# Longer estimates of when an attention task's results are there

## The chip, the cores and the metric
One core of a Trainium2 chip runs the whole program. The metric is device time in microseconds (us) of one execution. The engines are TensorE (PE, with its weight loads PEld), VectorE (DVE), ScalarE (ACT), GpSimd (POOL) and SyncE (SP, which issues most transfers); each takes its own instructions in order and waits where a result of another is not there yet.

## The reference
One transformer layer on 256 latent tokens and 256 context tokens, width 2048, in float32. What is computed:

```
h = rms_norm(x)*(1+sc_a)+sh_a;   hc = the same of the context           # adaLN modulation from c
p = h @ w_in                                                            # 2048 x 4928, split by head group
NA   (4 heads): neighbourhood attention with a bias, plus the context
GQA  (4 heads): q, k normed and rotated, 2 k/v heads
MLA  (4 heads): q = norm(cq) @ w_uq, k, v = norm(ckv) @ w_ukv, rotary part apart
DIFF (4 heads): softmax(q1 k1) - lam * softmax(q2 k2), times v, rms_norm per head
x = x + gt_a * (concat(heads) @ w_out)
x = x + gt_f * ((silu(h2 @ wg) * (h2 @ wu)) @ wd),  h2 = modulated norm of x
out = rms_norm(x)
```

## The kernel before
Every large product runs as three matmuls on split operands: `whi` is the weight cast on ACT (line 142), `wlo` the rest from DVE (line 145), and `mm3s` (lines 165, 166, 168) adds hi·hi, hi·lo and lo·hi into a PSUM tile `acc`. The weights come through eight buffers `raw`, issued by SP at line 128. The same eight buffers also carry rows of `w_ada` for the later modulation vectors (`mod_tasks`), which DVE sums at line 380.

Small work is written as Python generators, called tasks, and laid between these matmuls by the class `Side`, a planner that works when the program is built. It keeps a clock `now`. A task yields a cost and a wait: the planner moves `now` by the cost and takes up the task again only when `now` has passed the wait, its estimate of how long the other engines need. `pump(cost)` is called after each group of 12 large matmuls (some 2.6 on that clock), and steps the tasks that are due. `finish(tasks)` steps tasks until those named are done, with no large matmul written between. The framework then orders each engine's instructions by its own model and may draw a few later matmuls forward.

The order of the stage: the projections of NA and GQA in blocks; then `proj` for ML_CQ and DF_Q while the NA and GQA heads run as tasks `attend` (scores, softmax `soft`, transposes of `p` at line 607, product with v at line 658); `finish(*gq_tasks)` at line 814; `proj` for ML_CKV; the MLA up-projections `mla_up`; `proj` for DF_K; `finish(*ml_tasks)` at line 932; `proj` for DF_V; then the first twelve row blocks of `w_out` while the four DIFF heads run as tasks `diff`; `finish(*df_tasks)` at line 977; `split_o(3)`, which makes `o_hi3` (ACT, line 946) and `o_lo3` (DVE, line 947) of the DIFF heads' output; then the last four row blocks of `w_out`, which read them, and the second norm.

In `diff`, after the product with v (line 913), the result is squared (ACT 915), summed (DVE 917), turned into a factor (DVE 175, POOL 177), scaled (DVE 921) into `tok`, transposed (PE 607) and copied with the gain (ACT 923). `gq_prep` (lines 700 to 743) makes the rotated and normed q and k of GQA: the last two k tiles are transposed at line 607 and copied at line 742 into `gq_kT`, which the scores at line 748 read.

```
def finish(self, *tasks):
    ...
        self.now = max(self.now, best["ready"])
        self._step(best)
```

Of the kernel before, what the change touches and what calls it, by code (L numbers as in the profile page):

```python
# [87 lines left out]
def hybrid_dit_kernel(ctx: ExitStack, tc: tile.TileContext, a, out):  # L88
# [28 lines left out]
    def misc():  # L117
        return psM.tile([P, 512], F32, name="m")
# [61 lines left out]
    def tsl(t):  # L180
        return slice(t * P, (t + 1) * P)
# [393 lines left out]
    def tok():  # L575
        return at.tile([P, 512], F32, name="tok", bufs=4)
# [27 lines left out]
    def transposes(dst, src, n, evac=None):  # L604
        ps = misc()
        for j in range(n):
            pe.transpose(ps[:, tsl(j)], src[:, tsl(j)], ident)  # L607
        v = ps[:, :n * P].rearrange("p (j n) -> p j n", j=n)
        if evac is None:
            act.copy(dst, v)  # L610
        else:
            evac(dst, v)
# [16 lines left out]
    def soft(score, bias=None):  # L629

        if bias is not None:
            dve.tensor_tensor(out=score[:, 0:S], in0=score[:, 0:S], in1=bias, op=ALU.add)
        st = small.tile([P, 4], F32, name="st")
        dve.tensor_reduce(out=st[:, 0:1], in_=score, axis=AX.X, op=ALU.max, negate=True)
        p = at.tile([P, 512], F32, name="p", bufs=3)
        act.activation(p, score, AF.Exp, bias=st[:, 0:1], accum_out=st[:, 1:2])
        dve.reciprocal(st[:, 2:3], st[:, 1:2])
        return p, st[:, 2:3]

    def attend(h, g, score_mm, vt, v0, bias=None):  # L640
        pT = at.tile([P, 4, S], F32, name="pT", bufs=2)
        ps_ = []
        for t in range(2):
            sc = misc()
            score_mm(sc, h, t)
            p, r = soft(sc, None if bias is None else bias(h, t))
            if t < 1:
                act.activation(p, p, AF.Copy, scale=r)
            else:
                dve.tensor_scalar(out=p, in0=p, scalar1=r, scalar2=None, op0=ALU.mult)  # L650
            ps_.append(p)
            yield 0.9, (1.0 if t == 0 else 3.0)
        for t in range(2):
            transposes(pT[:, :, tsl(t)], ps_[t], 4)
            yield 0.43, (0.5 if t == 0 else 2.0)
        o = misc()
        for kc in range(4):
            pe.matmul(o[:, :S], lhsT=vt(kc)[:, v0:v0 + P], rhs=pT[:, kc, :], start=(kc == 0), stop=(kc == 3))  # L658
        act.copy(o_tile(g // 4)[:, g % 4, :], o[:, :S])
        yield 1.7, 0.0  # L660
# [45 lines left out]
    def gq_prep():  # L706
        q = {}
        yield 0.0, 3.0
        for t in range(2):
            r = head_rstd(gq_q[:, t, :], 4)  # L710
            q[t] = tok()
            rope(q[t], gq_q[:, t, :], tabs["q"][0][:, t, :], tabs["q"][1][:, t, :], 4, 128)
            qv = q[t].rearrange("p (h d) -> p h d", h=4)
            for h in range(4):
                dve.tensor_scalar(out=qv[:, h, :], in0=qv[:, h, :], scalar1=r[:, h:h + 1], scalar2=None, op0=ALU.mult)
            yield 0.0, 3.0
        gq_T["q"] = qtile()
        for t in range(2):
            transposes(gq_T["q"][:, :, tsl(t)], q[t], 4, scaled(128.0 ** -0.5))
            yield 0.43, 0.5  # L720
        k = {}
        for w in range(2):
            k[w] = tok()
            for i in range(2):
                t = 2 * w + i
                kw = k[w][:, i * S:(i + 1) * S]
                r = head_rstd(gq_k[:, t, :], 2)
                src = gq_k[:, t, :]
                if w == 0:
                    rope(kw, src, tabs["k"][0][:, t, :], tabs["k"][1][:, t, :], 2, 128)  # L730
                    src = kw
                for h in range(2):
                    dve.tensor_scalar(out=kw[:, tsl(h)], in0=src[:, tsl(h)], scalar1=r[:, h:h + 1], scalar2=None, op0=ALU.mult)
                yield 0.0, 2.0
        gq_T["k"] = kv.tile([P, 2, NT], F32, name="gq_kT", tag="gk")
        for t in range(4):
            src = k[t // 2][:, (t % 2) * S:(t % 2 + 1) * S]
            dst = gq_T["k"][:, :, tsl(t)]
            if t < 2:
                transposes(dst, src, 2)  # L740
            else:
                transposes(dst, src, 2, lambda d, v: act.activation(d, v, AF.Copy, scale=colB[:, 33:34]))
            yield 0.21, 0.5

    gq_ready = side.add(gq_prep(), lane="e", width=4)

# [27 lines left out]
    def cq_evac(t, ps):  # L774
        r = row_rstd(ps, 512)
        q = tok()
        dve.scalar_tensor_tensor(out=q, in0=ps, scalar=r[:, 0:1], in1=gcq, op0=ALU.mult, op1=ALU.mult)
        yield 0.0, 7.0
        transposes(None, q, 4, split_evac(cqT, tsl(t)))
        yield 0.43, 0.0  # L780

    def ckv_evac(t, ps):
        r = row_rstd(ps[:, 0:256], 256)
        k = tok()
        dve.scalar_tensor_tensor(out=k[:, 0:256], in0=ps[:, 0:256], scalar=r[:, 0:1], in1=gckv, op0=ALU.mult, op1=ALU.mult)
        if t < 2:
            rope(k[:, 256:320], ps[:, 256:320], c64[:, t, :], s64[:, t, :], 1, 64)
            dve.tensor_copy(k[:, 320:384], k[:, 256:320])
        else:
            act.copy(k[:, 256:320], ps[:, 256:320])  # L790
            act.copy(k[:, 320:384], ps[:, 256:320])  # L791
        yield 0.0, 7.0
        transposes(None, k, 2, split_evac(ckvT, tsl(t)))
        transposes(kpeT[:, tsl(t)].unsqueeze(1), k[:, 256:384], 1)
        yield 0.32, 0.0
# [4 lines left out]
    def dq_evac(t, ps):  # L800
        q = tok()
        rope(q, ps, c64[:, t, :], s64[:, t, :], 8, 64)
        yield 0.0, 7.0
        transposes(df_qT[:, :, tsl(t)], q, 4, scaled(0.125))
        yield 0.43, 0.0

# [60 lines left out]
    def dk_evac(t, ps):  # L867
        k = tok()
        if t < 2:
            rope(k, ps, c64[:, t, :], s64[:, t, :], 8, 64)  # L870
        else:
            act.copy(k, ps)
        yield 0.0, 7.0 if t < 2 else 2.0
        ps_ = misc()
        for j in range(4):
            pe.transpose(ps_[:, tsl(j)], k[:, tsl(j)], ident)
        for i in range(2):
            act.copy(df_kT[i][:, :, tsl(t)], ps_[:, i * S:(i + 1) * S].rearrange("p (j n) -> p j n", j=2))
        yield 0.43, 0.0
# [10 lines left out]
    def diff(h):  # L890
        pT = at.tile([P, 4, S], F32, name="pT", bufs=2)
        for t in range(2):
            ps_, rs_ = [], []
            for i in range(2):
                sc = misc()
                hb = slice(64 * i, 64 * i + 64)
                pe.matmul(sc, lhsT=df_qT[hb, h, tsl(t)], rhs=df_kT[h // 2][hb, h % 2, :], start=True, stop=True)  # L897
                p, r = soft(sc)
                ps_.append(p)
                rs_.append(r)  # L900
            yield 1.7, 0.5
            l1 = small.tile([P, 1], F32, name="l1")
            dve.tensor_tensor(out=l1, in0=rs_[1], in1=neglam, op=ALU.mult)
            dve.tensor_scalar(out=ps_[1], in0=ps_[1], scalar1=l1, scalar2=None, op0=ALU.mult)
            dve.scalar_tensor_tensor(out=ps_[0], in0=ps_[0], scalar=rs_[0], in1=ps_[1], op0=ALU.mult, op1=ALU.add)
            yield 0.0, 3.0 + 1.0
            transposes(pT[:, :, tsl(t)], ps_[0], 4)
            yield 0.43, 2.0 if t else 0.5
        vt = df_v["v"]
        o = misc()  # L910
        for t in range(2):
            for kc in range(4):
                pe.matmul(o[:, tsl(t)], lhsT=pT[:, kc, tsl(t)], rhs=vt[:, kc, tsl(h)], start=(kc == 0), stop=(kc == 3))  # L913
        sq = at.tile([P, 512], F32, name="ropet")
        act.activation(sq[:, :S], o[:, :S], AF.Square)
        ss = small.tile([P, 8], F32, name="ss")
        dve.tensor_reduce(out=ss[:, :2], in_=sq[:, :S].rearrange("p (h d) -> p h d", h=2), axis=AX.X, op=ALU.add)
        r = rstd_of(ss[:, :2], 2, P)
        od = tok()
        for t in range(2):  # L920
            dve.tensor_scalar(out=od[:, tsl(t)], in0=o[:, tsl(t)], scalar1=r[:, t:t + 1], scalar2=None, op0=ALU.mult)
        yield 1.7, 4.0
        transposes(o_tile(3)[:, h, :].rearrange("p (t n) -> p t n", t=2), od, 2, lambda d, v: act.activation(d, v, AF.Copy, scale=gsub))
        yield 0.21, 0.0

# [317 lines left out]
```

## Time and profile before

| | |
|---|---|
| time, median of 3 runs | 1356.57 us (1356.53 to 1358.23) |
| the profiled execution | 1355.29 us |
| its span, first to last instruction | 1353.5 us |
| PE busy | 1324.0 us, 98% |
| DVE busy | 923.2 us, 68% |
| ACT busy | 625.7 us, 46% |

The profile is of one execution; 1.8 us of its time lie outside its span. "Busy" of PE holds the pipelined end of each matmul, so short waits hide in it; the start times in a timeline show them. The blocks of attention tasks stand between 240 and 580 us of the span.

### The profile page before, as it was taken

Reading aid. Unit: us, or ns where it says so; the run is one execution under the profiler, and the core shown is the slowest. Engines: PE = TensorE matmul, PEld = TensorE weight load, DVE = VectorE, ACT = ScalarE, POOL = GpSimd, SP = SyncE. Lnnn points to the kernel's source line nnn. Section 1 sums busy time; section 2 is a strip of 40 time slices with the busy share of each in tenths; the row PEclk is TensorE's granted clock in tenths of the full one; section 3 lists DMA queues with packets and bytes.
Section 4 is the critical chain, followed back from the end, with each engine's and each line's share of the span. In section 5 each row is a group of like instructions: output and inputs, shape, how many; then the busy total and the mean of one; then the engine's idle time right before and its main releaser. Section 6 shows DMA issues by size and latency. Waiting matters only on the chain.

```text
span 1353.5 us, 21027 instructions
## 1 busy us (share of the span) xinstructions
PE 1324.0 (98%) x7018; PEld 1077.5 (80%) x7018; DVE 923.2 (68%) x1687; ACT 625.7 (46%) x1183; POOL 99.6 (7%) x159
## 2 busy tenths in 40 slices
PE   6999999999999999999999999999999999999997
PEld 4788888778886777777888888888888888888886
DVE  4577789998679747778887954445555566556565
ACT  4532343564334435557445444444444444444453
POOL 1110000100000000000322200001001000011000
PEclk9999999999999999999999999999999999999999
DMA  9999996586687756455999855567667655676553
GB/s 367 344 356 323 322 364 220 171 268 213 198 262 262 247 166 212 135 184 164 344 368 340 307 191 192 193 196 219 210 212 228 218 193 185 203 226 224 193 178 129
DMA packets 190161, 322.29 MB, mean 238 GB/s; under 512 B 22466, under 2 KB 62436, under 8 KB 189028
## 3 DMA queue, kind: packets, MB, share of 16 engines
q1 hardware_dynamic: 177568, 285.28, 63.8%
q0 software_dynamic: 9136, 32.53, 6.5%
q10 hardware_dynamic: 3348, 3.13, 0.7%
q8 instruction: 55, 0.90, 0.3%
q14 instruction: 54, 0.44, 0.1%
HBM read 314.56 MB, written 6.31 MB: 237 GB/s over the span
## 4 chain that ended last, share of the span: by engine, by line
PE 68%; DVE 1%; ACT 1%; DMA 0%; issue 0%; POOL 0%; POOLq 0%; DVEq 0%; SPq 0%; ACTq 0%
PE acc L165 21%; PE acc L168 21%; PE acc L166 21%; PE m L862 1%; PE m L607 1%; PE m L861 1%; PE m L913 1%; PE m L897 1%; PE m L658 1%; DVE wlo L145 0%; PE m L165 0%; PE m L166 0%; PE m L168 0%; ACT whi L142 0%; DMA raw<-in_w_out_dram 0%; PE m L385 0%
## 5 line engine op out<-in xcount | busy, mean ns | idle before, releaser
L145 DVE TENSOR_TENSOR wlo<-raw,whi 128x512 fp32r<-128x512 f32 (+1 forms) x764 | 490.4, 680 | 286.0 <-ACT whi L142 281.5
L142 ACT CAST whi<-raw 128x512 fp32r<-128x512 f32 (+1 forms) x764 | 437.6, 615 | 520.2 <-PE acc L166 427.5
L165 PE MATMUL acc<-whi,h_hi 128*128 128x512 f32 x704 | 274.2, 390 | 0.7 <-ACT h_hi L1013 0.7
L166 PE MATMUL acc<-whi,h_lo 128*128 128x512 f32 x704 | 274.1, 389 | 0.4 <-DVE h_lo L1014 0.4
L168 PE MATMUL acc<-wlo,h_hi 128*128 128x512 f32 x704 | 190.8, 390 | 0.0
L165 PE MATMUL acc<-whi,h 128*128 128x512 f32 (+1 forms) x416 | 161.6, 392 | 1.2 <-ACT tok L791 0.5
L166 PE MATMUL acc<-whi,h 128*128 128x512 f32 (+1 forms) x416 | 157.1, 379 | 0.0
L168 PEld LDWEIGHTS acc<-wlo,h_hi 128*128 128x128 f32 x704 | 132.1, 188 | 28.5 <-DVE wlo L145 1.2
L165 PEld LDWEIGHTS acc<-whi,h_hi 128*128 128x128 f32 x704 | 132.2, 188 | 28.2 <-ACT h_hi L1013 1.1
L166 PEld LDWEIGHTS acc<-whi,h_lo 128*128 128x128 f32 x704 | 132.2, 188 | 28.0 <-DVE h_lo L1014 0.7
L165 PE MATMUL acc<-whi,ah 128*128 128x512 f32 (+1 forms) x364 | 139.1, 384 | 0.0
L166 PE MATMUL acc<-whi,al 128*128 128x512 f32 (+1 forms) x364 | 138.6, 382 | 0.0
L380 DVE SCALAR_TENSOR_TENSOR ada_acc<-raw,cs,ada_acc 128x512 f32<-128x512 f32 x135 | 100.9, 747 | 21.7 <-DMA raw<-in_w_ada_dram 20.2
L168 PE MATMUL acc<-wlo,h 128*128 128x512 f32 (+1 forms) x416 | 114.5, 379 | 1.1 <-DVE wlo L145 1.0
L168 PE MATMUL acc<-wlo,ah 128*128 128x512 f32 (+1 forms) x364 | 96.2, 382 | 0.0
L165 PEld LDWEIGHTS acc<-whi,h 128*128 128x128 f32 x416 | 78.0, 188 | 19.2 <-issue 3.7
L166 PEld LDWEIGHTS acc<-whi,h 128*128 128x128 f32 x416 | 78.2, 188 | 13.4 <-issue 1.2
L168 PEld LDWEIGHTS acc<-wlo,h 128*128 128x128 f32 x416 | 75.9, 188 | 16.2 <-DVE wlo L145 2.5
L165 PEld LDWEIGHTS acc<-whi,ah 128*128 128x128 f32 x364 | 68.4, 188 | 13.3
L166 PEld LDWEIGHTS acc<-whi,al 128*128 128x128 f32 x364 | 68.5, 188 | 13.1
L168 PEld LDWEIGHTS acc<-wlo,ah 128*128 128x128 f32 x364 | 67.6, 188 | 13.3
L177 POOL TENSOR_TENSOR rstd<-ms,mhalf 128x1 f32<-128x1 f32 (+2 forms) x24 | 18.1, 755 | 513.5 <-DVE ms L175 513.5
(238 smaller groups left out, 1419.8 us busy)
## 6 DMA issues: line engine op xcount, KB each, us to landing
raw<-in_ffn_wg_dram SPq DMA_DIRECT2D x176, 256.0 KB, 2.8
raw<-in_ffn_wu_dram SPq DMA_DIRECT2D x176, 256.0 KB, 3.5
raw<-in_ffn_wd_dram SPq DMA_DIRECT2D x176, 256.0 KB, 3.7
raw<-in_w_in_dram SPq DMA_DIRECT2D x144, 256.0 KB, 4.7
raw<-in_w_ada_dram SPq DMA_DIRECT2D x144, 256.0 KB, 3.4
araw<-in_w_ada_dram SPq DMA_DIRECT2D x128, 256.0 KB, 5.1
raw<-in_w_out_dram SPq DMA_DIRECT2D x64, 256.0 KB, 3.4
graw<-in_w_ada_dram POOLq DMA_DIRECT2D x32, 512.0 KB, 6.1
```

What stands on the lines that cost most here:

```text
L142: act.copy(hi, raw_)
L145: dve.tensor_tensor(out=lo, in0=raw_, in1=hi.bitcast(F32), op=ALU.subtract)
L165: pe.matmul(dst, lhsT=l[0], rhs=r[0], start=start, stop=False)
L166: pe.matmul(dst, lhsT=l[0 if w_left else 1], rhs=r[1 if w_left else 0], start=False, stop=False)
L168: pe.matmul(dst, lhsT=l[1 if w_left else 0], rhs=r[0 if w_left else 1], start=False, stop=stop)
L177: pool.tensor_tensor(out=r[:, :n], in0=v[:, :n], in1=mhalf[:, :n], op=ALU.pow)
L380: dve.scalar_tensor_tensor(out=acc_, in0=part, scalar=cs[:, 0, kc:kc + 1], in1=acc_, op0=ALU.mult, op1=ALU.add)
L607: pe.transpose(ps[:, tsl(j)], src[:, tsl(j)], ident)
L658: pe.matmul(o[:, :S], lhsT=vt(kc)[:, v0:v0 + P], rhs=pT[:, kc, :], start=(kc == 0), stop=(kc == 3))
L861: pe.matmul(sc, lhsT=ml_qT[:, h, tsl(t)], rhs=ml_kT[:, h, :], start=True, stop=False)
L862: pe.matmul(sc, lhsT=qpeT[hb, h // 2, tsl(t)], rhs=kpeT[hb, :], start=False, stop=True)
L897: pe.matmul(sc, lhsT=df_qT[hb, h, tsl(t)], rhs=df_kT[h // 2][hb, h % 2, :], start=True, stop=True)
```

## The change
Only waits in `yield` statements change: those after the softmax, after transposes, after the norms and ropes of the projections and within `diff`. No instruction is added or taken away.

```diff
--- before.py
+++ after.py
@@ -649,10 +649,10 @@
             else:
                 dve.tensor_scalar(out=p, in0=p, scalar1=r, scalar2=None, op0=ALU.mult)
             ps_.append(p)
-            yield 0.9, (1.0 if t == 0 else 3.0)
+            yield 0.9, (1.0 if t == 0 else 6.0)
         for t in range(2):
             transposes(pT[:, :, tsl(t)], ps_[t], 4)
-            yield 0.43, (0.5 if t == 0 else 2.0)
+            yield 0.43, (1.0 if t == 0 else 3.5)
         o = misc()
         for kc in range(4):
             pe.matmul(o[:, :S], lhsT=vt(kc)[:, v0:v0 + P], rhs=pT[:, kc, :], start=(kc == 0), stop=(kc == 3))
@@ -717,7 +717,7 @@
         gq_T["q"] = qtile()
         for t in range(2):
             transposes(gq_T["q"][:, :, tsl(t)], q[t], 4, scaled(128.0 ** -0.5))
-            yield 0.43, 0.5
+            yield 0.43, 1.0
         k = {}
         for w in range(2):
             k[w] = tok()
@@ -731,7 +731,7 @@
                     src = kw
                 for h in range(2):
                     dve.tensor_scalar(out=kw[:, tsl(h)], in0=src[:, tsl(h)], scalar1=r[:, h:h + 1], scalar2=None, op0=ALU.mult)
-                yield 0.0, 2.0
+                yield 0.0, 4.0
         gq_T["k"] = kv.tile([P, 2, NT], F32, name="gq_kT", tag="gk")
         for t in range(4):
             src = k[t // 2][:, (t % 2) * S:(t % 2 + 1) * S]
@@ -740,7 +740,7 @@
                 transposes(dst, src, 2)
             else:
                 transposes(dst, src, 2, lambda d, v: act.activation(d, v, AF.Copy, scale=colB[:, 33:34]))
-            yield 0.21, 0.5
+            yield 0.21, (3.5 if t == 3 else 1.0)
 
     gq_ready = side.add(gq_prep(), lane="e", width=4)
 
@@ -775,7 +775,7 @@
         r = row_rstd(ps, 512)
         q = tok()
         dve.scalar_tensor_tensor(out=q, in0=ps, scalar=r[:, 0:1], in1=gcq, op0=ALU.mult, op1=ALU.mult)
-        yield 0.0, 7.0
+        yield 0.0, 10.0
         transposes(None, q, 4, split_evac(cqT, tsl(t)))
         yield 0.43, 0.0
 
@@ -789,7 +789,7 @@
         else:
             act.copy(k[:, 256:320], ps[:, 256:320])
             act.copy(k[:, 320:384], ps[:, 256:320])
-        yield 0.0, 7.0
+        yield 0.0, 10.0
         transposes(None, k, 2, split_evac(ckvT, tsl(t)))
         transposes(kpeT[:, tsl(t)].unsqueeze(1), k[:, 256:384], 1)
         yield 0.32, 0.0
@@ -800,7 +800,7 @@
     def dq_evac(t, ps):
         q = tok()
         rope(q, ps, c64[:, t, :], s64[:, t, :], 8, 64)
-        yield 0.0, 7.0
+        yield 0.0, 10.0
         transposes(df_qT[:, :, tsl(t)], q, 4, scaled(0.125))
         yield 0.43, 0.0
 
@@ -870,7 +870,7 @@
             rope(k, ps, c64[:, t, :], s64[:, t, :], 8, 64)
         else:
             act.copy(k, ps)
-        yield 0.0, 7.0 if t < 2 else 2.0
+        yield 0.0, 10.0 if t < 2 else 4.0
         ps_ = misc()
         for j in range(4):
             pe.transpose(ps_[:, tsl(j)], k[:, tsl(j)], ident)
@@ -903,9 +903,9 @@
             dve.tensor_tensor(out=l1, in0=rs_[1], in1=neglam, op=ALU.mult)
             dve.tensor_scalar(out=ps_[1], in0=ps_[1], scalar1=l1, scalar2=None, op0=ALU.mult)
             dve.scalar_tensor_tensor(out=ps_[0], in0=ps_[0], scalar=rs_[0], in1=ps_[1], op0=ALU.mult, op1=ALU.add)
-            yield 0.0, 3.0 + 1.0
+            yield 0.0, 6.0
             transposes(pT[:, :, tsl(t)], ps_[0], 4)
-            yield 0.43, 2.0 if t else 0.5
+            yield 0.43, 3.5 if t else 1.0
         vt = df_v["v"]
         o = misc()
         for t in range(2):
@@ -919,7 +919,7 @@
         od = tok()
         for t in range(2):
             dve.tensor_scalar(out=od[:, tsl(t)], in0=o[:, tsl(t)], scalar1=r[:, t:t + 1], scalar2=None, op0=ALU.mult)
-        yield 1.7, 4.0
+        yield 1.7, 6.0
         transposes(o_tile(3)[:, h, :].rearrange("p (t n) -> p t n", t=2), od, 2, lambda d, v: act.activation(d, v, AF.Copy, scale=gsub))
         yield 0.21, 0.0
```

In PE's order, before: the transposes of the last k tile of GQA (`tok_3212` into `m_3368`) and the first score with `gq_kT`.

```order
L607 MATMUL m_3368<-ident_67,tok_3212 128x128 x2
L165 MATMUL acc_3415<-whi_3421,h_322 128x512
L166 MATMUL acc_3415<-whi_3421,h_323 128x512
L165 MATMUL acc_3415<-whi_3425,h_322 128x512
L166 MATMUL acc_3415<-whi_3425,h_323 128x512
L165 MATMUL acc_3416<-whi_3421,h_322 128x512
L748 MATMUL m_3397<-gq_kT_3295,qT_3033 128x512
L748 MATMUL m_3406<-gq_kT_3295,qT_3033 128x512
```

After the change, in the same order, the end of the group that now stands between the transposes of the last k tile and that first score.

```order
L166 MATMUL acc_3339<-whi_3505,h_1118 128x512
L168 MATMUL acc_3338<-wlo_3503,h_1117 128x512
L168 MATMUL acc_3338<-wlo_3507,h_1117 128x512
L168 MATMUL acc_3339<-wlo_3503,h_1117 128x512
L168 MATMUL acc_3339<-wlo_3507,h_1117 128x512
L748 MATMUL m_3528<-gq_kT_3388,qT_3051 128x512
L748 MATMUL m_3537<-gq_kT_3388,qT_3051 128x512
```

Five large matmuls stood between the transposes and the score; now it is the whole group of twelve, of which the last five are seen.

In PE's order, before: the products with v (line 913) of DIFF heads 2 and 3, and what follows them.

```order
L168 MATMUL acc_6118<-wlo_6309,o_hi2_5624 128x512
L913 MATMUL m_6323<-v_5200,pT_6021 128x128 x8
L913 MATMUL m_6343<-v_5200,pT_6040 128x128 x8
L165 MATMUL acc_6369<-whi_6375,o_hi0_5616 128x512
L166 MATMUL acc_6369<-whi_6375,o_lo0_5617 128x512
```

After the change, at the same place; `o_hi3` and `o_lo3` are the split output of the DIFF heads.

```order
L168 MATMUL acc_6282<-wlo_6461,o_hi2_5624 128x512
L913 MATMUL m_6481<-v_5236,pT_6125 128x128 x8
L913 MATMUL m_6501<-v_5236,pT_6144 128x128 x8
L607 MATMUL m_6521<-ident_67,tok_6498 128x128 x2
L607 MATMUL m_6525<-ident_67,tok_6518 128x128 x2
L165 MATMUL acc_6553<-whi_6558,o_hi3_6545 128x512
L165 MATMUL acc_6594<-whi_6599,o_hi3_6545 128x512
L166 MATMUL acc_6553<-whi_6558,o_lo3_6546 128x512
L165 MATMUL acc_6553<-whi_6562,o_hi3_6545 128x512
```

Before, 72 of the 288 matmuls with the first twelve row blocks of `w_out` still followed the products: a group of twelve with the finished `o_hi0`, two transposes, another twelve, two more transposes, and the other 48. Now none is left: the four transposes follow at once, and the next large matmul reads `o_hi3`.

ACT's order at the same place, before: from the squares (line 915) to the split (line 946).

```order
L915 ACTIVATE ropet<-m 128x256 x2
L142 CAST whi<-raw 128x512 x2
L923 ACTIVATE oT<-m,gsub 128x256
L142 CAST whi<-raw 128x512 x2
L923 ACTIVATE oT<-m,gsub 128x256
L946 CAST o_hi_6545<-oT 128x1024
L142 CAST whi<-raw 128x512 x13
```

After the change, from the copies of the last `pT` on.

```order
L610 COPY pT<-m 128x4x128 x2
L915 ACTIVATE ropet<-m 128x256 x2
L923 ACTIVATE oT<-m,gsub 128x256 x2
L142 CAST whi<-raw 128x512
L946 CAST o_hi_6545<-oT 128x1024
L142 CAST whi<-raw 128x512 x11
```

Four weight casts stood between square and split; now there is one, and eleven stand behind the split.

## Rows read from the trace of the kernel before

**Rows 1.** Page, parts 1 and 4: busy time by engine; the last chain by engine.
```profile
PE 1324.0 (98%) x7018; PEld 1077.5 (80%) x7018; DVE 923.2 (68%) x1687; ACT 625.7 (46%) x1183; POOL 99.6 (7%) x159
...
PE 68%; DVE 1%; ACT 1%; DMA 0%; issue 0%; POOL 0%; POOLq 0%; DVEq 0%; SPq 0%; ACTq 0%
```
**Rows 2.** Waits of PE: instruction, releaser: us in total, times, longest us.
```profile
PE m L748 <- ACT gq_kT L742: 2.2, 1, 2.2
PE acc L168 <- DVE wlo L145: 1.0, 1, 1.0
PE acc L165 <- ACT whi L142: 0.9, 2, 0.6
...
PE acc L165 <- ACT tok L791: 0.5, 2, 0.3
...
PE m L607 <- DVE tok L785: 0.3, 1, 0.3
PE m L607 <- DVE p L650: 0.3, 1, 0.3
```
**Rows 3.** Windows: length; PE, PEld, DVE, ACT, POOL busy; PE clock, DMA share, GB/s.
```profile
20.00:25.00 5.00, 2.57 (x58) 1.94 (x55) 3.58 (x10) 3.78 (x8) 1.30 (x2) 1.00 1.08 408
25.00:30.00 5.00, 4.82 (x25) 4.38 (x26) 1.52 (x3) 1.86 (x2) 0.00 (x0) 0.66 1.01 418
250.00:300.00 50.00, 47.69 (x232) 36.69 (x231) 46.92 (x105) 33.93 (x76) 5.82 (x6) 1.00 0.71 228
580.00:590.00 10.00, 10.00 (x45) 8.26 (x44) 4.15 (x7) 3.23 (x5) 0.00 (x0) 1.00 0.56 182
590.00:600.00 10.00, 9.28 (x36) 6.26 (x35) 10.00 (x17) 7.26 (x14) 0.00 (x0) 1.00 0.48 151
```
**Rows 4.** Timeline of PE, first GQA score: start, us, instruction [idle before <-releaser].
```profile
283.15 0.38 PE L607 MATMUL m<-ident,tok 128*128 128x128 f32 x2
...
286.92 1.98 PE L748 MATMUL m<-gq_kT,qT 128*128 128x512 f32 x4 [2.23 <-ACT gq_kT L742]
```
**Rows 5.** Timeline of ACT at the same place.
```profile
285.88 0.62 ACT L142 CAST whi<-raw 128x512 fp32r<-128x512 f32 x1 [1.59 <-DMA raw<-in_w_in_dram]
286.40 0.47 ACT L742 ACTIVATE gq_kT<-m,colB 128x256 f32<-128x256 f32 x1
```
**Rows 6.** Timeline of PE, products of DIFF heads 2 and 3 and after.
```profile
569.80 3.73 PE L913 MATMUL m<-v,pT 128*128 128x128 f32 x32
573.29 0.48 PE L165 MATMUL acc<-whi,o_hi 128*128 128x512 f32 x1
...
579.10 0.38 PE L607 MATMUL m<-ident,tok 128*128 128x128 f32 x2
```
**Rows 7.** Timeline of DVE at the same place.
```profile
571.95 0.69 DVE L145 TENSOR_TENSOR wlo<-raw,whi 128x512 fp32r<-128x512 f32 x1
...
576.53 0.61 DVE L921 TENSOR_SCALAR tok<-m,rstd 128x128 f32<-128x128 f32 x2 [0.88 <-POOL rstd L177]
...
581.11 1.23 DVE L947 TENSOR_TENSOR o_lo<-oT,o_hi 128x1024 fp32r<-128x1024 f32 x1 [0.69 <-ACT o_hi L946]
```
**Rows 8.** Timeline of ACT, copy and split of the DIFF output.
```profile
579.52 0.48 ACT L923 ACTIVATE oT<-m,gsub 128x256 f32<-128x256 f32 x1 [0.46 <-PE m L607]
580.03 1.05 ACT L946 CAST o_hi<-oT 128x1024 fp32r<-128x1024 f32 x1
```
**Rows 9.** Timeline of ACT, casts for the last row blocks of w_out.
```profile
590.45 4.27 ACT L142 CAST whi<-raw 128x512 fp32r<-128x512 f32 x8 [5.66 <-PE acc L168]
595.99 0.62 ACT L142 CAST whi<-raw 128x512 fp32r<-128x512 f32 x1 [1.27 <-DMA raw<-in_w_out_dram]
```
**Rows 10.** Lines of DVE, 300 to 460 us: busy us, mean ns | idle before, releaser.
```profile
L380 DVE SCALAR_TENSOR_TENSOR ada_acc<-raw,cs,ada_acc 128x512 f32<-128x512 f32 x88 | 65.9, 749 | 14.5 <-DMA raw<-in_w_ada_dram 13.3
...
L650 DVE TENSOR_SCALAR p<-p,st 128x512 f32<-128x512 f32 x6 | 2.9, 478 | 0.0
```
**Rows 11.** Lines of ACT, whole span: busy us, mean ns | idle before, releasers.
```profile
L142 ACT CAST whi<-raw 128x512 fp32r<-128x512 f32 (+1 forms) x764 | 437.6, 615 | 520.2 <-PE acc L166 427.5 <-DMA raw<-in_w_in_dram 35.1 <-DMA raw<-in_ffn_wg_dram 11.9
```

## The prediction

> **What bounds the kernel now.** I read the page first. PE is busy for 98% of the span and the last chain runs over it for 68% [rows 1]; no other engine is near. So a change that moves instructions and adds none can gain only where PE waits, and loses where it makes PE wait anew. The second view is the list of PE's waits. Between 240 and 580 us, where the change acts, it holds little: 2.2 us before the first GQA score, 1.0 on a weight rest, and 0.3 to 0.9 on casts, copies and softmax results; all six rows together are 5.2 us [rows 2], of which 0.6 lies later, at 598 us, on a weight cast. That is the ceiling of the gain. The third view is the order of the changed kernel beside that of before, held against the timelines: it shows where PE now stands with nothing else to do. A large matmul starts each 0.22 us where PE is full (45 starts in 10 us, [rows 3]).
>
> **The change part by part.** All times are sums against the profiled execution, 1355.29 us, of which 1.8 lie outside the span.
>
> First GQA score. Before, the transposes of the last k tile started at 283.15 and the score at 286.92, with five large matmuls between and 2.2 us of waiting on the copy into `gq_kT` [rows 4]. The copy itself takes 0.5 us. It was late because ACT takes its work in order and stood for 1.6 us at a weight cast whose weights had not landed [rows 5]. Now twelve matmuls stand there: seven more, 7 x 0.22 = 1.5 us of cover. In ACT's new order two casts of weights and one `w_ada` row still stand ahead of the copy, so the cause is not removed, only covered. At least 0 is gained, if the weights are later by as much; at most 2.2. I take 1.9, near the top, since the copies of the tiles before it also stand earlier in ACT's queue.
>
> Other waits of the stage. The rows of 0.3 on `p`, 0.3 and 0.5 on `tok`, 0.3 (of 0.9) on a cast and 1.0 on a rest sum to 2.4 us [rows 2]. The first two are what longer estimates aim at; the other three wait on weights and on the release of accumulators, which the change does not touch. I take 0.5 gained, between 0 and 2.4.
>
> The finish of the GQA heads. Before, all four were done when it was reached; now all four are open, and two of them run score, softmax, transposes and product inside it. PE still has the scores, eight transposes of `df_qT` and 17 matmuls of ML_CKV, which the framework draws forward. On DVE a scaling of `p` (0.48 us) now stands behind rows of `w_ada` at 0.75 us each [rows 10], two between one scaling and the next, and the next weights' rests. Following DVE's order with those durations, each of the two scalings of `p` on DVE comes 0.5 to 0.9 us after PE could take it, 1.4 us by this estimate; but the same scalings ran behind the same kind of rows before, and the wait on them that shows is 0.3 [rows 2]. I go by that row, the nearest, and take 0.4 lost. From below it is 0; from above, SP now issues fourteen rows of `w_ada` in one piece ahead of the first ML_CKV weights, where it issued two to four: 14 x 0.75 = 10.5 us of DVE's time before the buffers come round. Of that the better part can pass while DF_Q still runs; I keep 4 us as the upper end.
>
> The finish of the MLA heads. Two heads ran inside it before, and PE lost nothing that a row shows. Now their transposes stand closer together and 28 rows of `w_ada` are issued in one piece. PE has eight scores and four products of its own there, so I take 0.3 lost, between 0.5 gained and 2 lost.
>
> The finish of the DIFF heads is the large term. Before, 72 large matmuls followed the products with v; now none does. So PE waits for the whole chain from these products to `o_lo3`. It can be read off the old trace. PE was free of the products at 573.29 [rows 6]. The second scaling on DVE ended at 576.53 + 0.61 = 577.1, with two weight rests of 0.6 to 0.7 us in its queue before it [rows 7]; the new order has none there, which saves 0.9 (between 0 and 1.3): 576.2. From the last transposes to the end of the copy with the gain it is 579.10 to 580.00, 0.9 us [rows 6, 8]: 577.1. One weight cast still stands before the split on ACT, 0.5 us [rows 5]: 577.6. From the start of the cast to `o_hi3` at 580.03 to the end of `o_lo3` at 582.34 it is 2.3 us [rows 7, 8]: 579.9. That is 6.6 us, in which PE has only four transposes and the two matmuls that need `o_hi3` alone, 0.8 us. So PE waits 5.8 us; between 4.5 and 7.
>
> What comes back. The last row blocks of `w_out` are read for half as many matmuls per weight, and PE starved there: 36 starts in 590 to 600 against 45 in the stretch before [rows 3], two of the 45 beside transposes, so about 8 x 0.22 = 1.8 us; ACT's casts came in a burst once their buffers were free and then waited 1.3 us for weights [rows 9]. Now the casts start when `o_hi3` is done, over a microsecond before PE resumes, and DVE's residual sums are out of the way. I take 1.4 back, between 0 and 1.8.
>
> The clock. In 20 to 25 us PE was busy for 2.57 of 5 us, and in the next 5 us the granted clock was 0.66 [rows 3]: of its two levels, 1.2 and 2.4 GHz, PE had the lower for part of it, and lost (1 - 0.66) x 5 = 1.7 us of work. The single wait of 2.2 us did not do that: the stretch 250 to 300 shows 1.00 [rows 3]. In the new wait PE has 0.8 us of work in 6.6, less than in 20 to 25. I take the fall and its 1.7 us; the other end is 0.
>
> The Trainium skill has a rule against the change here (TensorE: Matmul & The Clock Gate, section HAM oscillation — how this bites in real kernels): a wait for other engines' work between bursts can send the array back to half rate, so that the next burst starts slow. Its section Part 4: PE-mode transpose adds that in one kernel transposes did not count as work that keeps the rate up, so the four in this wait would not help. By both, the sum is the one below; if transposes count and are enough, it is 1.7 us less. The trace agrees with the first for the stretch at 20 us and has no wait like the new one; on the second no row here decides.
>
> The second norm. Its first transposes stand 8 large matmuls earlier in PE's order, 8 x 0.22 = 1.8 us, so PE may meet them before they are ready; most of that is work which then lies behind them. I take 0.3, between 0 and 1.8.
>
> Sum: -1.9 - 0.5 + 0.4 + 0.3 + 5.8 - 1.4 + 1.7 + 0.3 = +4.7 us. 1355.29 + 4.7 = 1360.0 us for an execution like the profiled one; the median of the runs lies 1.28 us above that one, so 1361.3 us is the forecast.
>
> **The rivals.**
>
> Not slower: the weights come in time. ACT waited 35.1 us in all for weights of the input projections [rows 11], and behind that queue stand most of the 4.6 us of waits that the change can reach (5.2 less the 0.6 at 598). SP's new order has the rows of `w_ada` in fewer, longer pieces, so that in the first half of the stage the weights stand closer to the front. If ACT's casts no longer wait there, all 4.6 goes; with no fall of the clock the sum is -4.6 + 0.4 + 0.3 + 5.8 - 1.4 + 0.3 = +0.8, 1357.4 us. It is faster than before as soon as the DIFF wait is under 5 us. For it speaks that the waits before the score come from a late weight; against it, that eight buffers and DVE's load (46.92 of 50 us busy, [rows 3]) stay as they are. Chance 0.24.
>
> The clock stays up: all else as forecast, 4.7 - 1.7 = +3.0, 1359.6 us. The four transposes and two matmuls fall inside the wait and may be enough. Chance 0.26.
>
> The GQA finish starves: the fourteen rows hold back the first ML_CKV weights and PE stands there for the 4 us of the upper end: 1361.3 + 3.6 = 1364.9 us. For it: DVE waited 13.3 us for rows of `w_ada` between 300 and 460 [rows 10]; against it, most of the fourteen are summed while DF_Q still runs. Chance 0.13.
>
> That the change does not act is excluded by the order: PE, DVE, ACT and SP all differ.
>
> **How the numbers follow.** The forecast has 0.37. Two tenths of a per cent, 2.7 us, is about what a measurement of this kernel can tell from no change: faster is under 1353.9, slower over 1359.3. Slower holds 0.36 of the forecast, the starved finish's 0.13 and 0.16 of the case without the fall, whose time lies just over the bound: 0.65. No change holds the other 0.01 and 0.10 of these, and 0.16 of the first rival: 0.27. Faster has the rest of the first rival: 0.08. The range goes from 1356.0, inside the first rival, to 1366.0, just over the starved finish.
>
> **What would show it.** The wait of PE on `gq_kT` at line 748 is under 0.5 us. In PE's timeline, right behind the 32 records of line 913 and the transposes of `tok`, the matmul with `o_hi3` starts some 5 us late, released by ACT line 946, and the next waits for DVE line 947. The clock reads below 1.00 in the 5 us behind it. The starts per 10 us behind it are 43 or more. It is wrong if that wait is under 3 us, if ACT's and DVE's work before it is finished early, or if PE shows new waits over 2 us between 300 and 460 us.

## The result: 1368.5 us, slower by 0.85%

The changed kernel took 1368.49 us (median; 1367.48 to 1372.12), beside 1356.55 for the kernel before: a ratio of 1.0085, 95% interval 1.0073 to 1.0097. The forecast of 1361.3 had the sign and missed the size; the time lies outside the range. The profiled execution took 1369.38 us, its span 1367.6.

A correction first: the three calls of `finish` that the sections above put at lines 814, 932 and 977 stand at lines 808, 926 and 971, and `gq_prep` starts at line 706.

The page of the changed kernel, parts 1 and 4. PE is busy for 1328.1 us where it was for 1324.0, but DVE and DMA now stand in the chain that ended last [rows 1]: it no longer runs over PE alone.

```profile
PE 1328.1 (97%) x7018; PEld 1082.5 (79%) x7018; DVE 923.9 (68%) x1687; ACT 624.9 (46%) x1183; POOL 99.5 (7%) x159
...
PE 81%; DVE 8%; DMA 7%; issue 2%; ACT 1%; POOL 1%; SPq 0%; ACTq 0%; POOLq 0%; DVEq 0%
```

PE's waits in the whole span of the changed kernel, as in [rows 2]. The wait at line 748 is gone. New are 6.5 us on a result of line 626, and two rows of 2.0 us each at the DIFF finish.

```profile
PE acc L165 <- DVE ropet L626: 6.5, 1, 6.5
...
PE acc L165 <- ACT o_hi L946: 2.0, 1, 2.0
PE m L607 <- DVE tok L921: 2.0, 2, 1.4
...
PE m L607 <- ACT df_kT L878: 1.0, 1, 1.0
```

Windows of the changed kernel, columns as in [rows 3].

```profile
250.00:300.00 50.00, 49.78 (x241) 39.92 (x240) 47.79 (x106) 32.60 (x69) 5.69 (x6) 1.00 0.78 250
...
360.00:365.00 5.00, 1.25 (x3) 1.09 (x4) 3.78 (x12) 0.47 (x2) 0.54 (x1) 0.70 0.67 206
365.00:370.00 5.00, 5.00 (x17) 3.92 (x17) 2.69 (x12) 0.65 (x3) 0.93 (x1) 0.62 0.35 80
...
600.00:605.00 5.00, 2.30 (x5) 1.40 (x6) 3.29 (x6) 3.94 (x8) 0.00 (x0) 0.59 0.16 46
605.00:610.00 5.00, 5.00 (x17) 3.92 (x17) 3.41 (x6) 3.21 (x7) 0.00 (x0) 0.72 0.71 218
610.00:620.00 10.00, 10.00 (x45) 8.03 (x44) 9.76 (x17) 6.08 (x14) 0.00 (x0) 1.00 0.75 226
```

In 250 to 300 PE is busy for 49.78 us, 2.1 more than before: the gain at the first GQA score. Between 100 and 1345 us the clock is below 1.00 in two places, 360 to 370 and 600 to 610 us; in the kernel before it was 1.00 there. In 610 to 620 there are 45 starts, where the same work had 36.

**The place that the prediction did not name.** PE's timeline at the end of ML_CKV in the changed kernel: its last accumulators are full at 356.6, and DF_K's first matmul, which needs one of them free, starts at 363.75. Its successors start each 0.42 us, the lower of the two levels, where a full PE starts one each 0.22.

```profile
356.64 0.60 PE L385 MATMUL m<-ident,ada_acc 128*128 128x128 f32 x4
363.75 0.77 PE L165 MATMUL acc<-whi,h 128*128 128x512 f32 x1 [6.50 <-DVE ropet L626]
364.31 0.63 PE L166 MATMUL acc<-whi,h 128*128 128x512 f32 x1
364.74 0.63 PE L165 MATMUL acc<-whi,h 128*128 128x512 f32 x1
```

DVE at the same place. The accumulator is freed by lines 785 to 626 of `ckv_evac`, and these stand behind two rows of `w_ada` (line 380). DVE takes its work in order and waited 2.79 us for the transfer of the first, after the 1.28 us of rests.

```profile
356.13 1.28 DVE L145 TENSOR_TENSOR wlo<-raw,whi 128x512 fp32r<-128x512 f32 x2
360.21 0.75 DVE L380 SCALAR_TENSOR_TENSOR ada_acc<-raw,cs,ada_acc 128x512 f32<-128x512 f32 x1 [2.79 <-DMA raw<-in_w_ada_dram]
361.26 0.75 DVE L380 SCALAR_TENSOR_TENSOR ada_acc<-raw,cs,ada_acc 128x512 f32<-128x512 f32 x1 [0.30 <-DMA raw<-in_w_ada_dram]
361.93 0.15 DVE L175 TENSOR_SCALAR ms<-ss 128x1 f32<-128x1 f32 x1
362.79 0.48 DVE L785 SCALAR_TENSOR_TENSOR tok<-acc,rstd,b_mla_gkv 128x256 f32<-128x256 f32 x1 [0.72 <-POOL rstd L177]
...
363.32 0.28 DVE L626 TENSOR_TENSOR ropet<-acc,rope_s 128x32 f32<-128x32 f32 x2
```

SP, which issues the transfers in order (second column: from the start of the first issue of the group to the end of the last, waits between them included). First the fourteen rows of `w_ada` that the finish of the GQA heads issues in one piece, from 296.12 to 309.85; then the place in question. The two rows are issued at 355.68, behind four of `mla_wuq` that held SP for 4.6 us, of which some 2.2 us is the issuing itself (0.55 us each) and the rest waiting.

```profile
296.12 13.73 SPq L128 DMA_DIRECT2D raw<-in_w_ada_dram  x14
...
350.14 0.80 SPq L128 DMA_DIRECT2D raw<-in_w_ada_dram  x2
350.99 4.60 SPq L819 DMA_DIRECT2D raw<-in_mla_wuq_dram  x4
355.68 1.04 SPq L128 DMA_DIRECT2D raw<-in_w_ada_dram  x2
```

DVE of the kernel before at the same place: no row of `w_ada` stands between the rests and the release.

```profile
353.94 1.29 DVE L145 TENSOR_TENSOR wlo<-raw,whi 128x512 fp32r<-128x512 f32 x2 [2.23 <-ACT whi L142]
356.01 0.15 DVE L175 TENSOR_SCALAR ms<-ss 128x1 f32<-128x1 f32 x1 [0.77 <-ACT ropet L765]
...
357.41 0.28 DVE L626 TENSOR_TENSOR ropet<-acc,rope_s 128x32 f32<-128x32 f32 x2
```

**The DIFF finish.** PE's timeline in the changed kernel, to be held against [rows 6].

```profile
594.12 3.73 PE L913 MATMUL m<-v,pT 128*128 128x128 f32 x32
598.42 0.59 PE L607 MATMUL m<-ident,tok 128*128 128x128 f32 x2 [0.57 <-DVE tok L921]
600.44 0.59 PE L607 MATMUL m<-ident,tok 128*128 128x128 f32 x2 [1.43 <-DVE tok L921]
...
603.04 0.80 PE L165 MATMUL acc<-whi,o_hi 128*128 128x512 f32 x1 [2.02 <-ACT o_hi L946]
604.08 0.80 PE L165 MATMUL acc<-whi,o_hi 128*128 128x512 f32 x1 [0.24 <-ACT whi L142]
```

The products end, counted as in the prediction, at 594.12 + 3.49 = 597.61; the first matmul with `o_hi3` starts 5.4 us later. The idle parts in the rows are 0.57 + 1.43 + 2.02 + 0.24 = 4.3 us. From 603.0 to 607.7 the matmuls are at the lower level, most with starts 0.42 us apart: nine of them, 9 x 0.2 = 1.8 us lost to the clock. DVE makes `o_lo3` at the same time:

```profile
603.02 1.23 DVE L947 TENSOR_TENSOR o_lo<-oT,o_hi 128x1024 fp32r<-128x1024 f32 x1 [0.25 <-ACT o_hi L946]
```

It ends at 604.25, 6.6 us after the products.

### The profile page after: what moved, and what is told of

Its sections match the earlier page's. It is cut to its first block, busy times and chain, and to the rows that moved or that the text cites. A ratio compares the mean times of both kernels' runs of the same rounds, so it can differ in the third digit from the quotient of the medians.

```text
span 1367.6 us, 21030 instructions
## 1 busy us (share of the span) xinstructions
PE 1328.1 (97%) x7018; PEld 1082.5 (79%) x7018; DVE 923.9 (68%) x1687; ACT 624.9 (46%) x1183; POOL 99.5 (7%) x159
## 4 chain that ended last, share of the span: by engine, by line
PE 81%; DVE 8%; DMA 7%; issue 2%; ACT 1%; POOL 1%; SPq 0%; ACTq 0%; POOLq 0%; DVEq 0%
PE acc L165 25%; PE acc L166 25%; PE acc L168 25%; DVE ada_acc L380 3%; DMA raw<-in_w_ada_dram 3%; PE m L301 1%; DMA raw<-in_w_in_dram 1%; DMA araw<-in_w_ada_dram 1%; DVE wlo L145 1%; PE m L607 1%; PE m L897 1%; DMA rowsB<-in_rows_dram 1%; POOL rstd L177 1%; DVE st L634 1%; PE m L658 1%
```

## The experiments

Theory A was formed from the rows above: two places cost, the DIFF finish, and the two rows of `w_ada` ahead of the release. Each run was timed beside the kernel before; ratios are to it.

**e1: the change without its DIFF part.**

```diff
-            yield 0.0, 6.0                      # 906
+            yield 0.0, 3.0 + 1.0
-            yield 0.43, 3.5 if t else 1.0       # 908
+            yield 0.43, 2.0 if t else 0.5
-        yield 1.7, 6.0                          # 922
+        yield 1.7, 4.0
```

> The changed kernel with the DIFF estimates (lines 906, 908, 922) as before. Theory A (two separate places: the finish of the DIFF heads, and the two w_ada rows that stand in VectorE's order ahead of the release of the ML_CKV accumulators, with transfers behind the rows of mla_wuq on SyncE): the DIFF waits (5.4 us) and the fall of the clock behind them (1.6 us) go and the starved last row blocks come back (+1 us), so 1368.5 - 6 = 1362.5 us; the wait of 6.5 us at line 165 near 363 us stays. Rival B (the DIFF heads are all of the loss): within 2 us of before, 1354 to 1358.

Measured: 1363.21 us, ratio 1.0041 (1.0026 to 1.0056). The DIFF waits are gone, the wait at the end of ML_CKV is still there, and longer. PE's timeline of e1:

```profile
366.60 0.77 PE L165 MATMUL acc<-whi,h 128*128 128x512 f32 x1 [7.85 <-DVE ropet L626]
```

**e2: the DIFF part alone** (the same three lines, the other way, in the kernel before).

> The kernel before with the DIFF estimates alone lengthened. Theory A: TensorE waits some 5.5 us for o_hi3 and o_lo3, the clock falls once behind that (1.6 us), about 1 us comes back: 1356.5 + 6 = 1362.5 us, and no wait over 1 us at the end of ML_CKV. Rival B (DIFF heads are all of the loss): 1367 to 1370.

Measured: 1362.68 us, ratio 1.0033 (1.0019 to 1.0048), 4.5 us. No wait on line 626 shows at the end of ML_CKV. The waits at the finish are those of the whole change, to 0.01 us:

```profile
593.19 0.59 PE L607 MATMUL m<-ident,tok 128*128 128x128 f32 x2 [0.57 <-DVE tok L921]
595.20 0.58 PE L607 MATMUL m<-ident,tok 128*128 128x128 f32 x2 [1.43 <-DVE tok L921]
597.80 0.80 PE L165 MATMUL acc<-whi,o_hi 128*128 128x512 f32 x1 [2.02 <-ACT o_hi L946]
```

So the DIFF heads are some 40% of the loss (4.5 of 11.5 us), and the rest does not need them: by e1 it is 5.6 us.

**e3 and e4: no step of `w_ada` during the last row block of ML_CKV**, in the whole change (e3) and without its DIFF part (e4).

```diff
-    tkv = proj(ML_CKV, 320, range(4), ckv_evac)
+    tkv = proj(ML_CKV, 320, range(4), ckv_evac,
+               lambda: side.lanes["gate"].update(width=0))
+    side.lanes["gate"].update(width=1)
```

> The changed kernel, in which no step of the w_ada tasks is taken during the last row block of ML_CKV (line 810), so that the two rows stand behind the first release of an accumulator instead of ahead of it; every other row in front is one that SyncE issues before mla_wuq. Theory A: the wait of 6.5 us and the second fall of the clock (1.6 us) go: 1368.5 - 8 = 1360.5 us. Rival C (the wait comes from the open GQA heads and DVE's load in general, the two rows only happen to stand there): the wait keeps at least 4 us, 1365 to 1369.

> Both: the DIFF estimates as before, and no w_ada step during the last row block of ML_CKV. Theory A: what is left of the change is the gain before the first GQA score (2.2 us) and small gains: 1356.5 - 2.5 = 1354 us, the clock at 1.00 from 300 to 640 us. Rival D (the longer estimates of the other tasks cost by themselves): 1357 or over.

Measured: e3 1364.35 us, ratio 1.0051 (1.0034 to 1.0069), so some 4.6 us of the 8 expected; e4 1358.06, ratio 1.0009 (0.9997 to 1.0020), no measurable difference instead of -2.5. In e3 too the wait was not gone but fell from 6.5 us to two, of 0.65 and 2.08 us, with the clock at 1.00 behind them. The rows moved only behind the first release, and the wait moved with them. PE and then DVE in e4:

```profile
356.88 0.47 PE L165 MATMUL acc<-whi,h 128*128 128x512 f32 x1 [1.30 <-DVE ropet L626]
362.20 0.76 PE L165 MATMUL acc<-whi,h 128*128 128x512 f32 x1 [2.10 <-DVE ropet L626]
```

```profile
356.46 0.28 DVE L626 TENSOR_TENSOR ropet<-acc,rope_s 128x32 f32<-128x32 f32 x2
358.54 0.75 DVE L380 SCALAR_TENSOR_TENSOR ada_acc<-raw,cs,ada_acc 128x512 f32<-128x512 f32 x1 [1.80 <-DMA raw<-in_w_ada_dram]
...
361.77 0.28 DVE L626 TENSOR_TENSOR ropet<-acc,rope_s 128x32 f32<-128x32 f32 x2
```

The first release is at 356.46. The row behind it waited 1.80 us for its transfer, so the second release came at 361.77 and PE waited 2.1 us for that. Rival C, a wait that the rows have nothing to do with, falls: the wait follows them. The clock behind e4's wait read 0.72 in 360 to 365 us.

**e7 and e12: the hold reaches to the first step of `mla_up`**, and the rows are ordered behind the releases; without the DIFF part (e7), and in the whole change (e12).

```diff
-    tkv = proj(ML_CKV, 320, range(4), ckv_evac)
+    tkv = proj(ML_CKV, 320, range(4), ckv_evac,
+               lambda: side.lanes["gate"].update(width=0))
     def mla_up():
+        side.lanes["gate"].update(width=1)
# ckv_evac, behind line 785:
+        newest[f"ckv{t}"] = nc.cur_bb.bb.instructions[-1]
# ada_block, line 380:
-                    dve.scalar_tensor_tensor(out=acc_, ...)
+                    with after(*[newest[n] for n in ("ckv2", "ckv3") if n in newest]):
+                        dve.scalar_tensor_tensor(out=acc_, ...)
```

> The changed kernel with the DIFF estimates as before, and the w_ada tasks held from the last row block of ML_CKV until the first step of mla_up, their rows on VectorE ordered behind the releases of the last two accumulators. Now no row with a late transfer stands ahead of any release. Theory A: the waits of 2.1 and 1.3 us that were left of the last try go too, and the fall of the clock: before - 2.5 us, ratio 0.998. Rival D (the longer estimates cost by themselves, or the rows come back late elsewhere): ratio 1.000 or over.

> The changed kernel whole, the DIFF estimates included, with the w_ada tasks held from the last row block of ML_CKV until the first step of mla_up and their rows on VectorE behind the releases of the last two accumulators. Theory A2: at the end of ML_CKV no wait over 0.5 us and no fall of the clock, so 8 us less than the changed kernel; the DIFF waits (5.4 us) and the fall of the clock behind them stay, so before + 4 us, as with the DIFF estimates alone (ratio 1.003). Rival E (something else of the change costs as well): before + 6 us or over.

Measured: e7 1356.39 us, ratio 0.9998 (0.9988 to 1.0008); e12 1362.21, ratio 1.0038 (1.0025 to 1.0052). In e7 nothing over 0.5 us is left there, and the clock stays at 1.00; PE's timeline:

```profile
356.19 0.47 PE L165 MATMUL acc<-whi,h 128*128 128x512 f32 x1 [0.32 <-ACT whi L142]
359.35 0.47 PE L165 MATMUL acc<-whi,h 128*128 128x512 f32 x1 [0.16 <-DVE ropet L626]
361.89 0.50 PE L165 MATMUL acc<-whi,h 128*128 128x512 f32 x1 [0.45 <-ACT tok L791]
```

Against e1 that is 1.0041 - 0.9998 = 0.0043, 5.8 us; against the whole change 1.0085 - 1.0038 = 0.0047, 6.4 us. This place, its fall of the clock included, is worth some 6 us of the 11.5. What is left in e12 agrees with e2. The gain that e7 was to show did not come: PE's waits on weight casts are 2.6 us in 240 to 680 us, where they were 0.9, as rival D allowed.

**e5, e6 and e9: one of the other parts alone** in the kernel before: the GQA preparation (lines 720, 734, 743), the evacuations (778, 792, 803, 873), the attention heads (652, 655), each with the change's numbers.

> The kernel before with the estimates of the preparation of the GQA heads alone lengthened (lines 720, 734, 743). The GQA heads then end in time, but the w_ada tasks fall differently: one row on ScalarE and one on VectorE, whose transfers SyncE issues behind mla_wuq, stand ahead of the first release of an ML_CKV accumulator. Theory A (these rows alone make the wait): the wait of 2.2 us before the first GQA score goes, a wait of 5 to 8 us at line 165 near 360 us comes, with a fall of the clock: before - 2 + 7 = before + 5 us. Rival C (the open GQA heads make it): no such wait, before - 2 us.

> The kernel before with the estimates of the projections' evacuations alone lengthened (lines 778, 792, 803, 873). As in the run with the GQA preparation alone, two rows with late transfers come to stand ahead of the first release. Theory A: a wait of 5 to 8 us and a fall of the clock near 360 us, the wait of 2.2 us before the first GQA score stays: before + 7 us. Rival C: within 1 us of before.

> The kernel before with the estimates of the attention heads alone lengthened (lines 652, 655). Two GQA heads are open at the finish on line 808, and the planner's clock stands 7.7 later behind it than before (285.5 against 277.7; 286.7 in the changed kernel, 279.8 with the GQA preparation alone). Theory A2 (the wait at the end of ML_CKV needs late w_ada rows ahead of the release, and its size follows how far the planner's clock has run ahead, since that sets how many rows stand before mla_wuq on SyncE): a wait of 4 to 8 us at line 165 near 360 us with a fall of the clock, before + 6 us. Rival E (the size depends on all parts together): under 2.5 us, before + 0 to 3 us.

Measured: e5 1355.47 us, ratio 0.9990 (0.9980 to 0.9999); e6 1359.66, 1.0013 (1.0002 to 1.0023); e9 1360.72, 1.0019 (1.0009 to 1.0029). For e5 and e6 theory A was wrong in size: two late rows stand ahead of the release, one of them on ACT (line 378), but the wait is 0.8 us in e5 and 2.0 in e6, not 5 to 8, and e6 lost 1.8 us where 7 were expected. That such rows stand there is needed, but how late they are is another thing. Rival C, that the open GQA heads make the wait, falls here again: by the planner's rules no GQA head is open at the finish in e6, which has the longer wait, and two are open in e5, which was expected to have none. For e9 a wait of 4 to 8 us was expected with that in mind, and PE's timeline shows 4.6:

```profile
362.47 0.76 PE L165 MATMUL acc<-whi,h 128*128 128x512 f32 x1 [4.63 <-DVE ropet L626]
```

The time of e9, 2.6 us over the kernel before, is not the 6 us of theory A2 but inside rival E's 0 to 3: the wait came as said, its price only in part.

What differs is how far the planner's clock has run when ML_CKV starts. `finish` sets that clock on to the due time of the next step, and the `w_ada` tasks fall due by it. Worked out from its rules it stands at 277.7 behind line 808 in the kernel before and in e6, 279.8 in e5, 285.5 in e9 and 286.7 in the whole change, for the same work of PE; the waits are 0.3, 2.0, 0.8, 4.6 and 6.5. More rows are then in the stage before the release. DVE's row of line 380 in 300 to 357 us (busy, mean ns, idle before), in the kernel before and in the changed one:

```profile
L380 DVE SCALAR_TENSOR_TENSOR ada_acc<-raw,cs,ada_acc 128x512 f32<-128x512 f32 x27 | 20.2, 748 | 6.8 <-DMA raw<-in_w_ada_dram 6.7
```

```profile
L380 DVE SCALAR_TENSOR_TENSOR ada_acc<-raw,cs,ada_acc 128x512 f32<-128x512 f32 x33 | 24.7, 748 | 12.4 <-DMA raw<-in_w_ada_dram 12.1
```

Six rows more, and 12.1 us of waiting for their transfers in place of 6.7. In between stand 28 in e5 and e6, and 30 in e9. The relation to the planner's clock is rough: the wait is large where the lead over the kernel before is 7.8 or more (e9, the whole change, e1), and 0.8 to 2.1 where it is 2.1 or less and late rows stand there (e5, e6 and, below, e10).

**e10: the planner's clock set back** behind that finish, without the DIFF part.

```diff
-    side.finish(*gq_tasks)
+    side.finish(*gq_tasks); side.now -= 8.0
```

> The changed kernel with the DIFF estimates as before, and the planner's clock set back by 8.0 behind the finish of the GQA heads (line 808), nothing else. Two late w_ada rows still stand ahead of the first release. Theory A2: the wait of 7.8 us at the end of ML_CKV falls to 1 to 2.5 us as in the runs with the GQA preparation or the evacuations alone; before + 0 us, from -2 to +2. Rival E: it keeps over 4 us, before + 4 to 6 us.

The planner's clock then leads the kernel before by 1.0. Measured: the wait is 2.1 us where e1 has 7.85, as theory A2 said, and 28 rows of line 380 stand in 300 to 357 us, as in e5 and e6:

```profile
PE acc L165 <- DVE ropet L626: 2.1, 1, 2.1
```

The time is 1359.67 us, ratio 1.0019 (1.0005 to 1.0033): 3 us less than e1, less than the wait gave back. The two waits are those of single executions, e10's the fastest of its kernel (1356.57 us) and e1's among the slowest (1365.96), so they are not to be set against the medians; one late row, on ACT, was still 2.05 us late, and the clock behind the wait read 0.84 and then 0.82. Where the rest is lost stays open, and the interval is wide.

**e8 and e11: attempts at a faster kernel.** e8 is e5 with the hold of e7; e11 has one number of the change.

```diff
-            yield 0.21, 0.5                         # 743, e11 only
+            yield 0.21, (3.5 if t == 3 else 0.5)
```

> The kernel before with the GQA preparation alone lengthened and the same hold of the w_ada tasks. Theory A: no wait before the first GQA score, none over 1 us at the end of ML_CKV: before - 2 us, ratio 0.9985. Rival C: the same. Rival D: 1.000 or over.

> The kernel before with one number of the change: the estimate for the last transposes of the k tile (line 743, t = 3) is 3.5 instead of 0.5. The rows of w_ada stand at the end of ML_CKV as before (none late ahead of a release). Theory A2: the wait of 2.2 us before the first GQA score shrinks to 1 us (five large matmuls more stand ahead of it), no wait there: before - 1 to - 2 us, ratio 0.999. Rival D: 1.000 or over, because the softmax copies or weights come late elsewhere.

Measured: e8 1359.84 us, ratio 1.0018 (1.0006 to 1.0030); e11 1357.15, ratio 0.9999 (0.9989 to 1.0008). For e8 rival D's case came: against e5 the hold cost 0.0028, 3.8 us. In both the wait moved to the softmax of a GQA head, as it did in e5 (1.9 us): e8 waits 1.5 us there, and e11's wait at line 748 fell from 2.2 to 0.2 us, and one of 2.0 us came on its `p`. PE's waits of e11:

```profile
PE m L607 <- ACT p L636: 2.0, 1, 2.0
...
PE m L748 <- ACT gq_kT L742: 0.2, 1, 0.2
```

e5 is the only version whose interval lies under 1, and only just. Why holding the rows made e5 slower was not settled.

## Why the prediction was wrong

- **First GQA score**, 1.9 gained: right in its window. The wait went, and PE is busy for 2.1 us more there. No time shows the gain, since e7, which has it and no wait at the end of ML_CKV, is at 0.9998. That such a wait can come back on the next result was seen only in e5 and e11.
- **The DIFF finish**, 5.8 lost: right in the mechanism and in the chain. `o_lo3` came 6.6 us after the products, as forecast, and the start of the first matmul with `o_hi3`, 5.4 us after the products, is what the chain read off the old trace gives (577.6 + 1.05 - 573.29 = 5.4). Only 4.3 us show as idle time, just under the range of 4.5 to 7: the rest is hidden, since the matmuls before `o_lo3` ran at the lower level of the clock and PE did not have to wait for it. So the sign that the next matmul waits for DVE line 947 did not come.
- **The clock**, 1.7 lost there: 1.8 measured. The case that the clock stays up did not come: it read 0.59 and 0.72 in 600 to 610 us, though the four transposes stand inside the wait. PE was busy for only 2.30 of the first 5 us, so this does not test the transposes by themselves. The Trainium skill's rule that was weighed (TensorE: Matmul & The Clock Gate, section HAM oscillation — how this bites in real kernels), that a wait between bursts can send the array back to half rate, agrees with the single wait of 6.50 us, behind which the granted clock read 0.70 and 0.62.
- **The weights that come back**, 1.4: 45 starts in place of 36, so up to 2. With the two terms before, the sum for DIFF is 6.1; e2 measured 4.5, with 6.1 inside its interval. The parts as measured are nearer: 4.3 + 1.8 - 2.0 = 4.1.
- **The finish of the GQA heads**, 0.4 lost, 4 at the upper end: this step failed. It held the right fact, that fourteen rows of `w_ada` are issued in one piece there, but looked for the price at the first ML_CKV weights and took 0.4 from the one row of the old trace. The fourteen rows were issued so, but PE waited there for no weight cast: all its waits on casts in 240 to 680 us are 0.2. The price came at the other end of ML_CKV, where rows with late transfers stand in DVE's order ahead of the release of accumulators: 6.5 us, and a second fall of the clock, some 6 us net by e1 and e7, and by e12. The rival that the finish starves PE (1364.9) named the rows of `w_ada` at that finish, but neither the mechanism (a release that stands behind late rows in an in-order queue), nor the place, nor the second fall.
- **Other waits and the MLA finish**, 0.2 gained together: e7 and e12 put all of the rest, the first term included, at about nothing; `df_kT` 1.0 us is the largest new one. So the gain of 2.4 us that the first GQA score and the other waits promised together shows in no time either.
- **The second norm**, 0.3 lost: no loss is seen. PE's waits at lines 1005, 1013 and 1014 sum to 1.3 us before and 1.0 after.
- Of the signs named in the prediction, the one that would make it wrong came: a new wait over 2 us between 300 and 460 us.

## What to carry to other kernels

An estimate in a planner moves not only the step that it belongs to: where a `finish` has to jump to a due time, the clock by which every other background task falls due jumps as well. So after an edit of waits, read the order of each in-order engine at every place where PE needs something released, and ask of each instruction ahead of the release when its transfer is issued. Background work that waits for memory is better ordered behind a release than ahead of it where it holds the release up: that took the wait away in e7 and e12. It is not free: on e5, whose wait was only 0.8 us, the same ordering cost 3.8 us (e8). And a wait removed at one place is a gain only if the next result is there in time (e11).

## What was not expected of the hardware

Whether a wait of about 2 us brings the clock down could not be told from its length. In the kernel before, 2.23 us without work left it at 1.00 [rows 3, 4]; in e6, a wait of 1.99 us was followed by a granted clock of 0.66, and in e2 one of 1.57 us likewise. The windows of e6 and of e2 behind these waits:

```profile
360.00:365.00 5.00, 5.00 (x18) 3.87 (x18) 3.50 (x12) 1.08 (x5) 0.92 (x1) 0.66 0.49 115
```

```profile
390.00:395.00 5.00, 4.89 (x22) 4.41 (x22) 2.39 (x7) 3.29 (x6) 0.00 (x0) 0.66 0.69 216
```

The nearest pairs say the same. PE's order is the same in e3 and e4 up to the DIFF heads, and at the same place 2.08 us without work left the clock at 1.00 in e3 (360 to 370 us), where 2.10 us in e4 was followed by 0.72. On the softmax of a GQA head, 2.01 us in e11 left it at 1.00, and 1.88 us in e5 was followed by 0.66.

The three waits of over 4 us at the end of ML_CKV were each followed by a clock below 1.00 in the next full 5 us: 0.62 in the whole change, 0.80 in e1, 0.81 in e9. What decides for the shorter ones stays open; the prediction's use of one wait of 2.2 us, as a sign that such waits leave the clock up, was too strong.
